# Other instruction durations in the scheduler of a two-layer hybrid trunk

## The chip, the cores and the metric

The kernel runs on one core of a Trainium2 chip. The metric is the device time of one execution in microseconds (us). The engines are TensorE (PE in the profile, its weight loads PEld), VectorE (DVE), ScalarE (ACT), GpSimd (POOL) and SyncE (SP), which issues all loads and stores.

## The reference

Two decoder layers over 512 tokens of 1024 features, all in float32. `rms_norm`, `rope`, `indexer`, `attention` and `mlstm` stand here for the reference's functions:

```
for i in range(2):
    xn = rms_norm(h, g_mix)
    c_q, k, v, k_idx, w_idx, mq, mk, mv, mo, mi, mf = split(xn @ w_in)
    c_q = rms_norm(c_q, g_cq)
    q, q_idx = rope(rms_norm(c_q @ w_q_up, g_qn)), rope(c_q @ w_iq_up)   # 8 heads of 64 each
    k, k_idx = rope(rms_norm(k, g_kn)), rope(rms_norm(k_idx, g_ik))
    score = sum over 8 heads of w_idx * relu(q_idx . k_idx), causal       # indexer
    sel   = the 128 best keys of each query by score
    att   = softmax(q . k over sel / 8) @ v                               # 8 heads, 2 kv heads
    hm    = sigmoid(mo) * rms_norm(mlstm(silu(conv(mq)), silu(conv(mk)), mv, mi, mf), g_mh)
    h = h + concat(att, hm) @ w_out
    h = h + relu(rms_norm(h, g_mlp) @ w_ff1) ** 2 @ w_ff2
    h = h + sigmoid(rms_norm(h, g_ple) @ w_ple_gate + b) * (p[i] @ w_ple)
return h
```

## The kernel before

The residual stream `h` stays on chip, feature-major, in eight tiles of 128 features by 512 tokens. Each float32 operand of a large product is split into a leading part (`hi`, made by ScalarE) and a remainder (`lo`, by VectorE, or for some weights by GpSimd if that is idle), both in float32r, and a product runs as three passes: hi x hi, hi x lo, lo x hi. Products of attention values, of the mLSTM and of sums of squares run in plain float32, which the trace shows as two matmul records each.

A weight tile is 128 x 1024. It is loaded by SyncE into `raw` (3 places), split into `hi` and `lo` (4 places each), and used for 24 products of 512 columns. In the trace, `lo<-raw,hi` is the remainder of a weight, `ps_proj` and `ps_up` are accumulators of projections, `ps_tr` of transposes and small sums, `ps_sc` of scores, `ps_po` of attention values, `ps_pn` of mLSTM values.

A layer's first part, `mix`, makes the compressed queries, then keys and gates, then the index queries and queries (`up`, 42 products of 512 columns a layer), whose norms (`headnorm`, lines 656 to 674) end with a gain that GpSimd multiplies in (`s<-s,const`, 128 x 512), followed by rope on VectorE and by `stack`, which splits them (`s_sp`) and has TensorE transpose them. From the index scores VectorE picks the 128 best keys in 16 rounds of MAX8 and MATCH_REPLACE8 for each of three query blocks. The mLSTM's values and output gates (label `values`, 192 products in one fixed order) and its queries and keys (label `conv`, eight blocks of 24 products) need none of that; they are what TensorE can do meanwhile. Then come attention, mLSTM, the output product in two halves, the MLP with 1536 products and the gated input.

No order is written out by hand. Class `Plan` records all instructions with their dependencies. `schedule` (lines 239 to 361) then simulates the five engines: whenever an engine is idle it takes, of the instructions that are ready and whose results have a place, the one with the highest rank. A rank is the longest chain of durations (`cost`, lines 199 to 227) and hops between engines (`lag`) behind the instruction, plus a fixed number of microseconds for its part of the work (`URGENT`); an earlier stage always goes first. An instruction that is offered to two engines goes to the one that is idle. The order in which this simulation issues the instructions is the program: each engine's queue executes in that order, and an instruction that is not ready holds up all behind it. So `cost` makes no instruction faster or slower; it moves instructions against one another.

The lines of `cost` for TensorE, where n is the number of columns and `single` means float32r:

```
if method == "transpose":
    return 56.0 if single else 109.0
return max(107.0, n / 2.4 + 3) if single else max(214.0, n / 0.6 + 3)
```

Of the kernel before, what the change touches and what calls it, by code (L numbers as in the profile page):

```python
"""Two layers of a hybrid trunk: top-k sparse attention next to mLSTM heads, squared-relu MLP, gated per-layer input.

The residual stream stays in SBUF, feature-major, for the whole program; every weight is read once.
A float32 product runs as three float32r passes: each operand is split exactly into a leading part of
12 significant bits and a remainder, and only the product of the two remainders (below float32's last bit)
is left to rounding.
"""
# [17 lines left out]
S = 512  # L25
# [10 lines left out]
# 500000 ** (-2 i / 16) in float32  # L36
INV_FREQ = (1.0, 0.1939227432012558, 0.03760603070259094, 0.007292664609849453, 0.0014142135623842478,
            0.00027424818836152554, 5.3182957344688475e-05, 1.0313385246263351e-05)
# columns of the feature-major constants
C_MIX, C_MLP, C_PLE, C_BPLE, C_CQ, C_CB, C_CW, C_MH, NCF = 0, 8, 16, 24, 32, 34, 42, 74, 78  # L40
# columns of the token-major constants
T_K, T_Q, T_I, T_F, NCT = 0, 192, 256, 260, 264
# tiles of the weight stream of one layer
W_CQ, W_UP, W_QK, W_V, W_O, W_OUT, W_FF1, W_FF2, W_PLE, W_GATE, NW = 0, 2, 4, 12, 16, 20, 28, 60, 92, 94, 102

# places of a room that must stay free behind an instruction that takes one
MARGIN = {"s": 5, "pw": 10, "out0": 0, "out1": 0, "mlstm": 8, "conv": 3}
# the first loads, in us of urgency from one to the next; the weights of the compressed queries come behind AHEAD of them
STEP, AHEAD = 5, 8
# how much more urgent a part of the work is than the length of the chain behind it says, in us  # L50
# [5 lines left out]
class View:  # L56
    """A part of a buffer, recorded: the steps that lead to it, and the elements it covers."""
# [25 lines left out]
    def split(self, inner):  # L83
        """[p, (a b)] -> [p, a, b] with b = inner."""
        return self._with(("rearrange", "p (a b) -> p a b", inner), self.index.reshape(-1, inner))

    def flat(self):
        """[p, a, b] -> [p, (a b)]."""
        return self._with(("rearrange", "p a b -> p (a b)", None), self.index.reshape(-1))
# [37 lines left out]
class Plan:  # L127
    """Records the program's instructions, chooses the order in which the engines issue them, and issues them.

    The order is that of a list scheduler: an idle engine takes, of the instructions whose operands are there and  # L130
    whose results have a place, the one with the longest chain of work behind it."""
# [16 lines left out]
    def add(self, forms):  # L148
        """forms: the instruction, possibly for several engines: (engine, method, args, kwargs)."""
# [48 lines left out]
    @staticmethod  # L198
    def cost(form):
        engine, method, args, kw = form  # L200
        out = kw["out"] if "out" in kw else args[0]
        views = [v for v in list(args) + list(kw.values()) if isinstance(v, View)]
        if engine == "sync":
            v = out if isinstance(out, View) else views[0]
            return 60.0 + v.index.size * v.shape[0] * 4 / 357.0
        n = max(v.index.size for v in views if v is not kw.get("accum_out"))
        columns = [v for v in views if v.index.size == 1 and n > 1]
        inputs = [v for v in views if v is not out and v.index.size > 1]
        bank = any(v.buf.room == "ps" for v in views)
        if engine == "tensor":  # L210
            single = (args[1] if len(args) > 1 else kw["lhsT"]).buf.dtype == F32R
            n = out.index.size
            if method == "transpose":
                return 56.0 if single else 109.0
            return max(107.0, n / 2.4 + 3) if single else max(214.0, n / 0.6 + 3)
        if engine == "scalar":
            return (51 if bank else 93) + n * 0.834 + 93 * len([v for v in columns if v is not out]) \
                + (0 if "accum_out" in kw and kw["accum_out"] is not None else 0)
        if engine == "gpsimd":
            return 100 + n * {"tensor_tensor": 2.25, "memset": 0.5, "affine_select": 1.0}.get(method, 1.4)  # L220
        if method == "reciprocal":
            return 69 + 6.25 * n
        if method == "tensor_tensor_scan":
            return 69 + 2.08 * n
        if method in ("tensor_copy", "tensor_scalar") and not bank and "accum_out" not in kw:
            return 69 + n * 0.52 + (61 if columns else 0)
        return 69 + n * 1.042 + (61 if columns and method == "scalar_tensor_tensor" else 0)

    @staticmethod
    def lag(a, b):  # L230
        """From the end of an instruction of engine a to the start of one of engine b that needs it."""
        if a == b:
            return {"vector": 110.0, "scalar": 60.0, "gpsimd": 100.0}.get(a, 0.0)
        if b == "sync":
            return 1220.0
        if a == "sync":
            return 900.0
        return 320.0 if b == "tensor" else 200.0 if a == "tensor" else 150.0
# [127 lines left out]
    def issue(self, nc, tc, pools):  # L366
        """pools: per room the Tile pool; a room without a number of places gives each buffer its own."""
# [25 lines left out]
class Trunk:  # L393
# [19 lines left out]
    def setup(self):  # L413
# [9 lines left out]
        # triu[s, t] = 1 where s <= t  # L423
# [3 lines left out]
        # cmask[q, s] = 0 where s <= q, else -1e30  # L427
# [4 lines left out]
        # negsel[r, h, :] = -1 where r == h  # L432
# [24 lines left out]
    def rope_tables(self):  # L457
        """cc = (cos, cos), sn = (-sin, sin) of position * inv_freq, token-major [128, 4, 16]."""
# [53 lines left out]
    def weight(self, ap, cols=1024, pool=False):  # L512
        """Loads a weight tile and splits it; returns (hi, lo)."""
# [16 lines left out]
    def rsqrt(self, v, shape):  # L530
        """v ** -0.5 of a tiny positive tile, to float32 accuracy."""
# [15 lines left out]
    def prep(self, l, gcol):  # L547
        """Splits h * gain per feature block and gathers the tokens' sums of squares."""
# [22 lines left out]
    def token_r(self, acc, dim):  # L571
        """acc [128 features, S] of squares -> [128 tokens, NTB] rsqrt(mean + eps)."""
# [14 lines left out]
    def wide_r(self, acc, dim):  # L587
        """acc [128 features, S] of squares -> rsqrt(mean + eps) of every token, on every partition, [128, S]."""
# [16 lines left out]
    def spread(self, r):  # L605
        """[128 tokens, NTB] -> the same value on every partition, [128, S]."""
# [18 lines left out]
    def mm3(self, out, w, x, first, last):  # L625
        """out += w^T x, w and x given as (hi, lo)."""
        nc = self.nc
        head = nc.tensor.matmul(out, w[0], x[0], start=first, stop=False)
        nc.tensor.matmul(out, w[0], x[1], start=False, stop=False)
        return head, nc.tensor.matmul(out, w[1], x[0], start=False, stop=last)  # L630

    def token_step(self, o, w, cols, x, k, per, tb, first, last):
        """o [128 tokens of block tb, cols] += x_k^T w_k; a tile w holds `per` k-blocks."""
# [7 lines left out]
    def rope(self, x, heads, blocks=range(NTB)):  # L641
        """In place on the first 16 dims of x: per token block [128, heads, 64]."""
# [13 lines left out]
    def headnorm(self, x, heads, gain, per_head):  # L656
        """x: per token block [128, heads, 64] (in place): rms norm of each head, times gain."""
# [18 lines left out]
    def stack(self, y, tb, outs):  # L676
        """y [128 tokens of block tb, 8 heads, 64] -> outs[head][:, block]: the leading parts of the 64 dims on
        partitions 0..63, the remainders on 64..127."""
# [18 lines left out]
    def doubled(self, x, heads):  # L697
        """x: per token block [128, heads, 64] -> per head (hi, lo) tiles [128, S], the 64 dims twice on the
        partitions."""
# [17 lines left out]
    def blocks(self, ws, xs, t=slice(0, S)):  # L717
        """Blocks of 128 output features side by side; the last feature block of x comes last."""
# [7 lines left out]
    def mix(self, l):  # L726
# [6 lines left out]
        # compressed queries  # L733
# [33 lines left out]
        # keys, values, indexer key and weights, gates  # L767
# [19 lines left out]
        # index queries and queries  # L787
# [52 lines left out]
        # gates of the mLSTM, token-major [128, NTB, 4]  # L840
# [22 lines left out]
        # log1p(z) = 2 y (1 + lp)  # L863
# [4 lines left out]
        # before[tb] = sum of the blocks ahead of tb  # L868
# [26 lines left out]
        # values and output gates of the mLSTM, token-major  # L895
# [21 lines left out]
        # mLSTM queries and keys: convolution over tokens, silu (times two)  # L917
# [18 lines left out]
        # attention  # L936
# [113 lines left out]
    def out_half(self, l, half, cat):  # L1050
        """Adds a half of the output product (0: mLSTM, 1: attention) to the residual stream."""
# [12 lines left out]
    def inputs(self, l, i, raws):  # L1064
        """Half of the product of the per-layer input, for the end of the layer; fills gaps of the tensor engine."""
# [69 lines left out]
    def ple(self, l):  # L1135
# [7 lines left out]
        for n0, cnt in ((0, 2), (2, 1), (3, 1), (4, 1), (5, 1), (6, 1), (7, 1)):  # L1143
            ws = [self.wtile(l, W_GATE + n0 + j) for j in range(cnt)]
            # the very last block in two halves of the tokens: less is left to do behind its last product
# [51 lines left out]
def col_blocks(w):  # L1197
    """[l, K, N] -> [l, N/128, 128, K]: per block of 128 columns, the rows of each 128-row block side by side."""
# [4 lines left out]
def row_pairs(w):  # L1203
    """[l, K, N] -> [l, K/256, 128, 2 N]: two 128-row blocks side by side."""
# [4 lines left out]
def out_pairs(w):  # L1209
    """[l, 512, 1024] -> [l, 4, 128, 1024]: two blocks of 128 columns side by side, each with its 128-row blocks."""  # L1210
    return col_blocks(w).reshape(L, 4, 2, 128, 512).transpose(0, 1, 3, 2, 4).reshape(L, 4, 128, 1024)


def columns(v):
    """[l, N] -> [l, 128, N/128]."""
# [42 lines left out]
```

## Time and profile before

| | |
|---|---|
| Time, median of 3 runs | 1372.2 us (1370.88 to 1372.2) |
| Span of the profiled execution, from its first to its last instruction | 1370.7 us, 1.5 us less than the median |
| TensorE busy | 1333.6 us, 97% |
| VectorE, ScalarE, GpSimd busy | 887.2, 554.8, 188.1 us |
| Loaded and stored | 116.40 MB, mean 85 GB/s |
| Chain that ended last | TensorE 88%, VectorE 8%, ScalarE 2% |

All instructions carry line 381, where `issue` calls them, so they are told apart by their tiles. Busy time of TensorE is modelled with overlapping ends: one 512-column product is shown as some 390 ns long, while the next starts 231 ns after it. Starts are therefore the better measure of its pace. The two layers have the same plan, and what stands at 72 us in layer 0 stands at 748 us in layer 1.

### The profile page before, as it was taken

To read this page: it belongs to the slowest core of one execution; us is meant where nothing else is said; L and a number is where in the kernel's file an instruction comes from. 1 tells how busy PE (TensorE), PEld (TensorE's weight loads), DVE (VectorE), ACT (ScalarE), POOL (GpSimd) and SP (SyncE) were. 2 spreads that over 40 slices of the span, in tenths; PEclk is the share of its full clock that TensorE was granted. 3 is DMA by queue.
4 is the path that set the end of the run, shared out by engine and by line. 5 is a ranking of instruction groups with operands and counts; after the bars stand their busy time and mean duration, and the time that the engine had idled before them with its cause. 6 is when DMAs were issued, how large, how long until landed. Compare 5 with 4: busy or idle time off the path is not lost.

```text
span 1370.7 us, 17012 instructions
## 1 busy us (share of the span) xinstructions
PE 1333.6 (97%) x6336; PEld 1096.2 (80%) x6336; DVE 887.2 (65%) x1791; ACT 554.8 (40%) x1106; POOL 188.1 (14%) x151
## 2 busy tenths in 40 slices
PE   7979999999999999999998899999999999999998
PEld 6767889888888888888896778988888888888887
DVE  7989998575354453554859999966743534535454
ACT  4765486332122221234546644844222212222441
POOL 4244200120000000012104341003100000000210
PEclk9989999999999999999999899999999999999999
DMA  5212211333333233333231123103223233323321
GB/s 189 70 55 78 92 32 32 93 92 92 96 95 101 93 92 92 93 100 96 80 90 50 66 83 93 32 21 102 93 93 93 93 97 99 97 93 92 95 83 69
DMA packets 34355, 116.40 MB, mean 85 GB/s; under 512 B 4192, under 2 KB 4704, under 8 KB 34272
## 3 DMA queue, kind: packets, MB, share of 16 engines
q1 hardware_dynamic: 34272, 115.32, 27.4%
q8 instruction: 49, 0.80, 0.2%
q14 instruction: 34, 0.28, 0.1%
HBM read 113.21 MB, written 2.10 MB: 84 GB/s over the span
## 4 chain that ended last, share of the span: by engine, by line
PE 88%; DVE 8%; ACT 2%; issue 1%; DMA 1%; POOL 0%; SPq 0%; ACTq 0%; DVEq 0%; POOLq 0%
PE ps_proj L381 78%; PE ps_sc L381 3%; PE ps_tr L381 3%; DVE s L381 3%; PE ps_po L381 2%; PE ps_pn L381 1%; ACT s L381 1%; DVE s_w L381 1%; DVE wide L381 1%; DVE s_sp L381 1%; DVE m L381 1%; DVE tiny L381 1%; DVE lo L381 0%; POOL s L381 0%; DMA raw<-wa 0%
## 5 line engine op out<-in xcount | busy, mean ns | idle before, releaser
L381 PE MATMUL ps_proj<-s,hi 128*128 128x512 f32 x2960 | 920.1, 393 | 0.4 <-ACT hi L381 0.4
L381 PEld LDWEIGHTS ps_proj<-s,hi 128*128 128x128 f32 x2960 | 554.3, 188 | 127.0 <-issue 1.8
L381 PE MATMUL ps_proj<-s,lo 128*128 128x512 f32 (+1 forms) x1480 | 576.9, 393 | 0.3 <-DVE lo L381 0.3
L381 ACT ACTIVATE hi<-raw 128x1024 fp32r<-128x1024 f32 (+1 forms) x212 | 222.4, 1052 | 646.2 <-PE ps_proj L381 317.3
L381 PEld LDWEIGHTS ps_proj<-s,lo 128*128 128x128 f32 x1480 | 278.2, 188 | 64.1 <-DVE lo L381 0.7
L381 DVE TENSOR_TENSOR lo<-raw,hi 128x1024 fp32r<-128x1024 f32 (+1 forms) x181 | 223.2, 1234 | 33.9 <-ACT hi L381 30.9
L381 DVE TENSOR_TENSOR const<-const,ps_proj 128x512 f32<-128x512 f32 x96 | 66.0, 688 | 224.3 <-PE ps_proj L381 224.3
L381 POOL TENSOR_TENSOR lo<-raw,hi 128x1024 fp32r<-128x1024 f32 x31 | 75.6, 2442 | 531.9 <-ACT hi L381 525.0
L381 DVE SCALAR_TENSOR_TENSOR s_v<-ps_proj,s 128x512 f32<-128x512 f32 x64 | 43.9, 691 | 138.3 <-PE ps_proj L381 138.3
L381 POOL TENSOR_TENSOR s<-s,s 128x512 f32<-128x512 f32 x42 | 68.3, 1626 | 411.5 <-ACT s L381 297.0
L381 PE MATMUL ps_proj<-hi,s 128*128 128x512 f32 (+1 forms) x384 | 112.4, 381 | 7.2 <-ACT hi L381 7.2
L381 PE MATMUL ps_sc<-s,s 128*128 128x384 f32 (+3 forms) x288 | 85.4, 382 | 0.0
L381 PEld LDWEIGHTS ps_proj<-hi,s 128*128 128x128 f32 x384 | 69.3, 194 | 16.3 <-ACT hi L381 7.2
L381 PE MATMUL ps_proj<-lo,s 128*128 128x512 f32 (+1 forms) x192 | 66.5, 385 | 1.9 <-DVE lo L381 1.9
L381 PEld LDWEIGHTS ps_sc<-s,s 128*128 128x128 f32 x288 | 52.5, 195 | 9.4 <-issue 3.1
L381 ACT ACTIVATE s<-ps_tr 128x128 fp32r<-128x128 f32 (+2 forms) x170 | 38.9, 307 | 34.4 <-PE ps_tr L381 34.1
L381 DVE MATCH_REPLACE8 s<-m,s 128x384 f32<-128x384 f32 (+2 forms) x96 | 51.2, 537 | 0.0
L381 DVE TENSOR_TENSOR s<-s_vv,s 128x512 fp32r<-128x512 f32 x64 | 49.2, 773 | 0.2
L381 PE MATMUL ps_po<-at,s_et 128*128 128x64 f32 x320 | 48.9, 254 | 0.0
L381 DVE MAX8 m<-s 128x8 f32<-128x384 f32 (+2 forms) x96 | 48.8, 542 | 0.0
L381 PEld LDWEIGHTS ps_po<-at,s_et 128*128 128x128 f32 x320 | 47.8, 191 | 1.1
L381 DVE SCALAR_TENSOR_TENSOR s<-const,const,s 128x512 fp32r<-128x512 f32 x48 | 39.8, 833 | 11.5 <-ACT s L381 11.4
(133 smaller groups left out, 1105.0 us busy)
## 6 DMA issues: line engine op xcount, KB each, us to landing
raw<-ws SPq DMA_DIRECT2D x204, 512.0 KB, 3.5
raw<-wa SPq DMA_DIRECT2D x8, 336.0 KB, 3.4
const<-xt SPq DMA_DIRECT2D x8, 256.0 KB, 4.7
out<-const SPq DMA_DIRECT2D x7, 256.0 KB, 2.0
s<-pt SPq DMA_DIRECT2D x4, 256.0 KB, 4.1
const<-ct SPq DMA_DIRECT2D x2, 132.0 KB, 4.2
out<-const SPq DMA_DIRECT2D x2, 128.0 KB, 1.7
const<-cf SPq DMA_DIRECT2D x2, 39.0 KB, 2.7
```

Source lines behind the costliest of these rows:

```text
L381: ins = getattr(getattr(nc, e), method)(*[value(x) for x in args], **{k: value(x) for k, x in kw.items()}).ins
```

## The change

Six numbers in `cost` are changed. Nothing else that acts is: comments and docstrings have become blank lines, so line numbers stay.

```
         if engine == "tensor":
             ...
             if method == "transpose":
-                return 56.0 if single else 109.0
-            return max(107.0, n / 2.4 + 3) if single else max(214.0, n / 0.6 + 3)
+                return 60.0 if single else 109.0
+            return max(111.0, n * 0.4375 + 7) if single else max(172.0, n * 1.66 + 11)
         ...
         if engine == "gpsimd":
-            return 100 + n * {"tensor_tensor": 2.25, "memset": 0.5, "affine_select": 1.0}.get(method, 1.4)
+            return 100 + n * {"tensor_tensor": 2.4, "memset": 0.8, "affine_select": 1.0}.get(method, 1.4)
```

## Rows read from the trace of the kernel before

**Rows 1.** The page: busy time, share of the span and instructions of each engine.

```profile
span 1370.7 us, 17012 instructions
PE 1333.6 (97%) x6336; PEld 1096.2 (80%) x6336; DVE 887.2 (65%) x1791; ACT 554.8 (40%) x1106; POOL 188.1 (14%) x151
```

**Rows 2.** Busy time by stage: stretch, length, engines' busy us, clock, DMA share, GB/s.

```profile
0.00:20.00 20.00, 10.96 (x55) 10.01 (x56) 15.58 (x14) 15.18 (x24) 14.82 (x24) 1.00 0.66 209
20.00:40.00 20.00, 19.28 (x94) 16.35 (x93) 14.02 (x66) 6.04 (x9) 0.00 (x0) 0.91 0.41 123
...
73.00:80.00 7.00, 0.00 (x0) 0.00 (x0) 7.00 (x4) 0.00 (x0) 5.68 (x3) 0.71 0.30 81
80.00:130.00 50.00, 47.18 (x222) 37.58 (x222) 47.09 (x122) 30.69 (x86) 18.34 (x13) 0.94 0.24 73
130.00:165.00 35.00, 35.00 (x155) 27.82 (x156) 33.09 (x84) 17.20 (x28) 13.59 (x11) 1.00 0.29 91
165.00:235.00 70.00, 70.00 (x506) 63.01 (x505) 65.79 (x224) 51.98 (x167) 3.39 (x8) 1.00 0.11 31
235.00:675.00 440.00, 440.00 (x1902) 356.46 (x1901) 231.22 (x280) 133.18 (x168) 34.22 (x21) 1.00 0.31 93
...
911.00:1366.00 455.00, 454.69 (x1994) 370.56 (x1992) 234.69 (x288) 130.18 (x164) 30.59 (x18) 1.00 0.29 91
1366.00:1371.00 5.00, 0.00 (x0) 0.00 (x0) 1.00 (x3) 0.51 (x1) 0.00 (x0) 0.85 0.09 31
```

**Rows 3.** The chain that ended last, in order of time: start us, us, what.

```profile
221.24 2.23 PE ps_pn L381 x20
...
284.21 361.49 PE ps_proj L381 x1560
```

**Rows 4.** TensorE in order of time, around its long wait in either layer.

```profile
72.55 0.40 PE L381 MATMUL ps_proj<-lo,s 128*128 128x512 f32 x1
80.14 0.62 PE L381 MATMUL ps_tr<-const,s_sp 128*128 128x128 f32 x3 [7.19 <-DVE s L381]
...
755.57 0.62 PE L381 MATMUL ps_tr<-const,s_sp 128*128 128x128 f32 x3 [7.22 <-DVE s L381]
```

**Rows 5.** VectorE in order of time, layer 0.

```profile
64.03 2.29 DVE L381 TENSOR_TENSOR wide<-wide,wide 128x32 f32<-128x32 f32 x1
66.36 0.19 DVE L381 SCALAR_TENSOR_TENSOR wide<-wide,wide 128x32 f32<-128x32 f32 x1
...
71.60 1.30 DVE L381 TENSOR_TENSOR s_w<-s,const 128x64 f32<-128x64 f32 x1 [1.17 <-POOL s L381]
...
74.11 2.35 DVE L381 TENSOR_TENSOR s_w<-s,const 128x64 f32<-128x64 f32 x1
```

**Rows 6.** GpSimd in order of time, layer 0.

```profile
63.85 2.42 POOL L381 TENSOR_TENSOR lo<-raw,hi 128x1024 fp32r<-128x1024 f32 x1 [10.35 <-ACT hi L381]
68.88 5.16 POOL L381 TENSOR_TENSOR s<-s,const 128x512 f32<-128x512 f32 x3 [2.60 <-DVE tiny L381]
73.99 4.69 POOL L381 TENSOR_TENSOR lo<-raw,hi 128x1024 fp32r<-128x1024 f32 x2
```

**Rows 7.** TensorE by stage, layer 0: products into ps_proj alone, then ps_up alone.

```profile
40.00:73.00 33.00, 17.36 (x66) 1.00 0.24 75
80.00:130.00 50.00, 37.12 (x138) 0.94 0.24 73
...
40.00:73.00 33.00, 9.95 (x42) 1.00 0.24 75
```

**Rows 8.** TensorE's short waits, 80 to 130 and 756 to 806 us: total, times, longest.

```profile
PE ps_tr L381 <- DVE s_sp L381: 2.7, 3, 1.3
...
PE ps_tr L381 <- DVE s_sp L381: 2.6, 3, 1.3
```

**Rows 9.** GpSimd's groups from 60 to 130 us: busy us, mean ns | idle before.

```profile
L381 POOL TENSOR_TENSOR lo<-raw,hi 128x1024 fp32r<-128x1024 f32 x9 | 21.8, 2431 | 38.1 <-ACT hi L381 34.6 <-issue 3.4
L381 POOL TENSOR_TENSOR s<-s,const 128x512 f32<-128x512 f32 x4 | 6.5, 1637 | 3.2 <-DVE tiny L381 2.6 <-DVE s L381 0.6
```

## The prediction

> **What bounds the kernel now.** I read the totals of the page first, then the busy time by stage, then the chain of waits, then the three engines around the one place where TensorE stands. The totals show TensorE busy for 97% of the span [rows 1]. The stages show where the other 3% lie [rows 2]: TensorE is full from 130 to 716 us and again from 806 to 1366 us, and is short only in the first 40 us, at 40 to 130 us (layer 0, indexer) and at 716 to 806 us (the same in layer 1). In a full stretch the order of the instructions can't matter: 1560 products of 512 columns take 361.49 us, 231.7 ns each, whatever lies between them [rows 3]. So the change is worth what it does in the two indexer stretches, and there VectorE is full: 7.00 of 7 us while TensorE does nothing, 47.09 of the 50 after it.
>
> At 72.9 us TensorE's queue reaches transposes whose operands VectorE has not made, and waits 7.19 us; 675 us later it waits 7.22 us in the same place [rows 4]. The work behind them in the queue can't pass. VectorE is late because of GpSimd: a 128x32 TENSOR_TENSOR takes 2.29 us where its neighbour of that size takes 0.19 us, and small ones after it take 1.30 and 2.35 us [rows 5]. Each of the long ones lies over a GpSimd TENSOR_TENSOR: three gains of the queries for 5.16 us from 68.88, and two remainders of weights for 4.69 us behind them [rows 6]. The scheduler's table has no such stretching: 69 + 32 x 1.042 is 102 ns for that 2.29 us instruction. So the plan believes VectorE faster than it is.
>
> The Trainium skill (SBUF — State Buffer, section "SBUF: two separate sides") says that VectorE instructions with two SBUF inputs and GpSimd ones lock each other out for a whole instruction. The 2.29 us agree. By that rule the block's 9.85 us (5.16 + 4.69) are lost to such VectorE instructions wherever it stands, so a split block only spreads the wait and the sum stays at the +3.0 us below; by the rows alone, where two blocked instructions take 1.3 us only, a split could give up to the 7.2 us of the wait back. The chance of that case is set from the rows.
>
> **The change part by part.** No instruction is added or removed, so its direct cost is zero; everything is in the order, on all five queues. SyncE's loads only follow the plan, and DMA has room (a share of at most 0.41 after the first 20 us [rows 2]).
>
> *TensorE, 512-column float32r products: 216.3 to 231 ns.* The new figure is what the trace has (231.7 ns), the old one 15 ns short. The cover it gave: the scheduler hands TensorE a fill product whenever nothing more urgent is ready, and an instruction that needs VectorE enters the queue when the plan thinks VectorE done. With products too short by 6%, the plan put 6% more of them ahead of every such instruction, and on the chip that excess absorbed part of VectorE's unplanned delay. With the true figure fewer stand ahead, while VectorE's delay, which the table still doesn't know, stays. So TensorE arrives at the blocked transposes earlier and waits longer, and the displaced products come later. How much: from 40 to 73 us the trace has 66 products into ps_proj and 42 into ps_up, and 138 into ps_proj from 80 to 130 [rows 7]. At 14.7 ns each (231 - 216.3; a few have 336 columns and move by 11) that is 1.6 us before the long wait and 2.0 us between the short waits behind it, 3.6 us in layer 0 at most. Layer 1 runs the same plan, so the upper end is 7.2 us for both. Lower end nothing: the short waits after the stall, 2.7 and 2.6 us [rows 8], and those before it could swallow the displaced products. Below nothing this term by itself can't go, since it only takes fill away. I take the middle, 3.6 us, as the long waits, three quarters of the waiting, can't be refilled behind the blocked head and the short ones partly can.
>
> *GpSimd: 2.25 to 2.4 ns an element.* 512 columns go from 1252 to 1329 ns, 1024 from 2404 to 2558; the trace has 1637 for the gains and 2431 for the remainders between 60 and 130 us [rows 9]. The plan now sees what waits for GpSimd later: 0.08 us for each of 4 gains, 0.15 for each of 9 remainders, 1.7 us a layer if all were in one chain. This works against the first term (the dependents move back in the queues), but few lie in one chain with TensorE's waits. Bounds -1.7 to 0 us a layer; I take -0.3, or -0.6 in all, by the three gains that run before the long wait (0.23 us).
>
> *TensorE, float32.* Products of 64 columns or fewer go from 214 to 172 ns, 128-column ones from 216 to 223.5, 129 from 218 to 225 (trace: 20 records, two a product, in 2.23 us, 223 ns [rows 3]). These run where TensorE is full, 165 to 235 us [rows 2], so no wait moves directly; cost zero. What could go wrong there: VectorE is also nearly full (65.79 of 70 us), and attention put later could leave TensorE without work before the output product. Bounds 0 to +3 us a layer, by the size of the short waits; I take 0.
>
> *Urgencies.* The scheduler orders by the longest chain behind an instruction. The chain of mLSTM values has 192 products a layer, so its head gains 192 x 14.7 = 2.8 us; the queries lose up to 80 x 42 = 3.4 us from the chain of attention products and regain 0.6 us from the scores. So weights for the fill products move up by some 3 to 6 us against the queries, which can change which of a remainder and a gain GpSimd runs first. This is the part I can't follow to the end: it can merge or split the block of five GpSimd instructions. From the row, the most at stake in a layer is the long wait, 7.2 us, plus what the halved clock after it costs: the granted clock averages 0.94 over the 50 us from 80 [rows 2], which is 6 us at 1.2 GHz and so 3 us of work. Bounds -10 to +7 us a layer; I take 0, since the block is made of the same instructions released in the same chain.
>
> *Start and end.* The first 40 us lose 9 and 0.7 us to loads and first splits [rows 2], and the last 5 us have no product left; order changes little there: bounds -1 to +1 us, taken as 0.
>
> Sum: 3.6 - 0.6 = +3.0 us on the profiled span of 1370.7 us. The median of the runs shown is 1372.2, 1.5 us above the span; I carry that along: 1370.7 + 1.5 + 3.0 = 1375.2, rounded to 1375.
>
> **The rivals.** A difference below 0.2% (2.7 us) can't be told from no change here.
>
> First rival, nothing measurable: the waits are set by VectorE and GpSimd, whose order in the stretch stays, and the displaced products fall into the short waits. For it: the two layers repeat the wait to 0.03 us [rows 4], so it is made by the dependency chain. Against it: VectorE works at its limit for 100 us, so a displaced product has no idle time guaranteed. 1370 to 1375; centre 1372.
>
> Second rival, faster: the changed urgencies let a weight's remainder run before the gains, or spread the gains, so that the block of five GpSimd instructions breaks, VectorE's instructions slip through and the long wait halves in both layers: -7.2 us, 1365. It decides from the point where one GpSimd remainder moves out of the ten microseconds after 68.88 us; if the wait goes entirely and the clock stays up, 2 x 10 = 20 us, 1352. For it: the values move up by as much as the queries go down. Against it: the remainders wait for ScalarE's leading parts (38.1 us of GpSimd's idle time [rows 9]), so urgency alone doesn't bring them earlier.
>
> Third rival, clearly slower: the block grows by another remainder (2.4 us a layer) and attention finishes late, 3 us a layer: 2 x 5.4 = 11 on top of the 3, 1386. For it: VectorE is full up to 235 us. Against it: TensorE shows no wait there now.
>
> **How the numbers follow.** Forecast, slower by 0.2 to 0.7%: 0.36, with 1375. Nothing measurable: 0.27. Faster: 0.29, most of it from 1362 to 1369. Clearly slower: 0.08. So faster 0.29, same 0.27, slower 0.44. The range of 8 in 10 runs from 1362 (leaving out a tenth, where the long waits vanish) to 1385 (leaving out the upper part of the third rival); the forecast's own range is 1375 to 1382.
>
> **What would show it.** Right: both long waits of TensorE for VectorE are still there, near 8 us each, at the same kind of transposes, fewer products into ps_proj stand before them, GpSimd runs gains and remainders back to back, and full stretches keep 231 to 232 ns a product. The first term is wrong if the long waits get shorter while the GpSimd block is unchanged; the rival of the urgencies is right if the block is split and the clock no longer falls behind it. The whole is wrong if a wait appears where TensorE is full now, at 130 to 716 or 806 to 1366 us, or if the start moves by more than a microsecond.

## The result and the profile after

The changed kernel takes 1417.76 us (1417.67 to 1420.34, 4 runs) against 1372.2 us: the ratio is 1.0337, 95% interval 1.0322 to 1.0351. That is 45.6 us slower, where 3 us slower and a range up to 1385 us were forecast.

First the totals of the page, as in [rows 1]:

```profile
span 1416.0 us, 17028 instructions
PE 1354.8 (96%) x6336; PEld 1103.7 (78%) x6336; DVE 911.1 (64%) x1807; ACT 551.7 (39%) x1096; POOL 185.1 (13%) x145
```

TensorE's idle time has grown from 37.1 to 61.2 us. The other 21 us stand as busy time of the same 6336 products; part of it is time at the halved clock, for which an estimate stands below. Next the busy time by stage, columns as in [rows 2]; the indexer stretch is one window here:

```profile
20.00:40.00 20.00, 16.27 (x85) 13.96 (x86) 13.99 (x67) 6.16 (x9) 0.00 (x0) 1.00 0.34 110
40.00:130.00 90.00, 77.63 (x385) 61.39 (x383) 86.49 (x238) 54.10 (x161) 34.90 (x19) 0.96 0.22 68
130.00:165.00 35.00, 35.00 (x147) 26.55 (x146) 35.00 (x88) 16.35 (x28) 15.31 (x14) 1.00 0.28 91
165.00:190.00 25.00, 20.74 (x102) 15.16 (x100) 24.87 (x52) 13.53 (x29) 1.08 (x2) 1.00 0.24 67
190.00:240.00 50.00, 48.35 (x350) 44.41 (x350) 40.63 (x147) 33.90 (x113) 1.47 (x5) 0.93 0.07 21
240.00:262.00 22.00, 17.82 (x96) 14.17 (x96) 11.46 (x40) 7.81 (x25) 0.13 (x1) 0.84 0.00 1
```

Four of these windows of the kernel before, the first one the indexer stretch again (20 to 40 and 130 to 165 us stand in [rows 2]):

```profile
40.00:130.00 90.00, 78.28 (x386) 62.52 (x385) 85.12 (x245) 57.15 (x165) 35.60 (x24) 0.94 0.24 75
165.00:190.00 25.00, 25.00 (x147) 21.10 (x146) 24.93 (x82) 18.01 (x56) 2.08 (x4) 1.00 0.14 43
190.00:240.00 50.00, 50.00 (x385) 45.97 (x385) 43.72 (x149) 35.57 (x115) 1.31 (x4) 1.00 0.08 22
240.00:262.00 22.00, 22.00 (x97) 17.85 (x96) 11.00 (x13) 5.21 (x7) 0.00 (x0) 1.00 0.32 97
```

The reader is to see that the indexer stretch, on which the prediction was built, has hardly more idle time (12.4 us against 11.7), and that the loss stands behind it, at 165 to 262 us, where TensorE was full before and is now idle 10.1 us. The 3.0 us more of idle time from 20 to 40 us make nothing late: the last product of the keys, with which that part ends, starts at 42.2 us before and 42.7 after. Layer 1 has the same picture 700 us later.

Matching each product of the two traces by its place in the program gives the sizes in layer 0. The last product of the mLSTM values starts at 131.1 us before and 134.2 after (+3.1). The last attention product starts at 231.6 and 242.2, so 7.5 us more were lost on the way. The first MLP product starts at 277.9 and 300.1, so another 11.6 us were lost. In layer 1 `mix` takes 263.7 us before and 287.0 after: +23.3, beside +22.2. Outside `mix` nothing has changed: the long stretch of products keeps its pace of [rows 3], 231.5 ns each, in the chain that ended last:

```profile
306.18 361.59 PE ps_proj L381 x1562
```

What TensorE waits for in the new places is in the view of its waits from 165 to 262 us (total, times, longest); before, this view has no line:

```profile
PE ps_sc L381 <- DVE s L381: 2.7, 1, 2.7
PE ps_tr L381 <- DVE s_hn L381: 2.5, 1, 2.5
PE ps_sc L381 <- DVE s_d L381: 2.4, 3, 1.0
```

The cause is fill that is left over: work that TensorE could do while it waits, done too late to serve for that. Products into ps_proj in two stretches of layer 0, before and then after; up to 230 us these are the conv blocks:

```profile
165.00:190.00 25.00, 14.09 (x56) 1.00 0.14 43
190.00:230.00 40.00, 0.00 (x0) 1.00 0.10 28
```

```profile
165.00:190.00 25.00, 12.35 (x44) 1.00 0.24 67
190.00:230.00 40.00, 9.64 (x24) 0.91 0.04 12
```

Before, all conv blocks are done at 188 us, when attention gets going. After, the last block of 24 products is still to do at 190 us and, ranked below attention, is scattered between its products until 221.6 us. The fourth mLSTM head needs that block. Its products into ps_pn move from 221 to 243 us, behind the last attention product, and its norm, which before lay under attention, now has only the first products of the output half beside it.

This order is made by the plan and not first on the chip. In TensorE's queue 35 of layer 0's 240 attention instructions stand ahead of the last conv product before, 130 in the changed kernel. `schedule` itself, run on the old table, never leaves TensorE idle in layer 0's `mix` and starts the last conv product at 152 us of its own clock. Run on the new one, it starts that product at 185 us and leaves TensorE idle for 5.3 us between the last values product and the last attention product and for 5.9 us behind it, 11.2 us in all. The simulation knows nothing of VectorE's stretched instructions [rows 5], so idle time of this size needs none of them.

TensorE in order of time around that norm:

```profile
250.03 0.40 PE L381 MATMUL ps_proj<-s,lo 128*128 128x512 f32 x1
252.96 1.16 PE L381 MATMUL ps_tr<-const,s_hn 128*128 128x128 f32 x4 [2.53 <-DVE s_hn L381]
254.90 1.58 PE L381 MATMUL ps_proj<-s,hi 128*128 128x512 f32 x2 [0.78 <-ACT s L381]
...
259.26 1.05 PE L381 MATMUL ps_proj<-s,hi 128*128 128x512 f32 x2
...
260.51 0.63 PE L381 MATMUL ps_proj<-s,hi 128*128 128x512 f32 x2
```

The gaps are small, but after them the granted clock falls to the 1.2 GHz level (0.84 as a mean of the 22 us): a pair of products takes 1.05 us there, and 0.63 us once the clock is back at 260.5 us. By the clocks of the table above, 0.93 over 50 us and 0.84 over 22 us, the halved clock takes up to 7.0 us a layer from 190 to 262 us, an estimate; with the 10.1 us of idle time that is most of the 19.1 us lost behind the values.

### The profile page after: what moved, and what is told of

It is laid out like the page before. It is cut to its first block, busy times and chain, and to the rows that moved or that the text cites. A ratio compares the mean times of both kernels' runs of the same rounds, so it can differ in the third digit from the quotient of the medians.

```text
span 1416.0 us, 17028 instructions
## 1 busy us (share of the span) xinstructions
PE 1354.8 (96%) x6336; PEld 1103.7 (78%) x6336; DVE 911.1 (64%) x1807; ACT 551.7 (39%) x1096; POOL 185.1 (13%) x145
## 4 chain that ended last, share of the span: by engine, by line
PE 78%; DVE 17%; issue 2%; ACT 2%; DMA 1%; POOL 0%; SPq 0%; DVEq 0%; ACTq 0%; POOLq 0%
PE ps_proj L381 69%; DVE s L381 8%; DVE m L381 3%; PE ps_sc L381 3%; PE ps_tr L381 2%; PE ps_po L381 2%; DVE s_sp L381 2%; PE ps_pn L381 1%; DVE tiny L381 1%; DVE wide L381 1%; DVE lo L381 1%; ACT hi L381 0%; DVE s_d L381 0%; ACT s L381 0%; DVE s_t L381 0%
## 5 line engine op out<-in xcount | busy, mean ns | idle before, releaser
L381 PEld LDWEIGHTS ps_proj<-s,hi 128*128 128x128 f32 x2960 | 555.9, 189 | 131.1 <-ACT s L381 3.0
L381 DVE TENSOR_TENSOR lo<-raw,hi 128x1024 fp32r<-128x1024 f32 (+1 forms) x185 | 227.1, 1229 | 33.1 <-ACT hi L381 30.1
L381 PE MATMUL ps_proj<-hi,s 128*128 128x512 f32 (+1 forms) x384 | 115.3, 385 | 7.3 <-ACT hi L381 7.3
L381 PE MATMUL ps_sc<-s,s 128*128 128x384 f32 (+3 forms) x288 | 88.9, 398 | 14.2 <-DVE s L381 5.4
L381 POOL TENSOR_TENSOR lo<-raw,hi 128x1024 fp32r<-128x1024 f32 x27 | 67.6, 2503 | 106.5 <-ACT hi L381 98.2
L381 ACT ACTIVATE s<-ps_tr 128x128 fp32r<-128x128 f32 (+2 forms) x170 | 39.1, 310 | 37.1 <-PE ps_tr L381 37.1
L381 PEld LDWEIGHTS ps_po<-at,s_et 128*128 128x128 f32 x320 | 50.7, 203 | 2.6
L381 DVE MAX8 m<-s 128x8 f32<-128x512 f32 (+2 forms) x96 | 48.8, 543 | 0.0
L381 ACT ACTIVATE s<-const,const 128x512 fp32r<-128x512 f32 x48 | 34.2, 714 | 29.7 <-DVE const L381 27.8
```

The lines of the kernel that those rows point to most:

```text
L381: ins = getattr(getattr(nc, e), method)(*[value(x) for x in args], **{k: value(x) for k, x in kw.items()}).ins
```

## The experiments

The table's values are used twice: for the ranks (the chain behind an instruction) and for the simulated clock (when an engine is free again). The first two runs take these apart. Both give `cost` a second argument:

```
 c = min(self.cost(f, RANK) for f in op.forms)      # e1: new table, e2: old
 op.end = now + self.cost(op.form, CLOCK)           # e1: old table, e2: new
```

> The new durations are used for the ranks alone (the chains of work behind an instruction), the old ones for the simulated clock. Theory A, pace: the harm comes from the simulated clock, which lets TensorE do fewer fill products (values, conv) before attention is ready; then attention, which ranks higher, pushes the last conv blocks and the last mLSTM heads behind it. By A this kernel is near the kernel before: 1366 to 1382 us, the last products of the fourth mLSTM head (ps_pn) before the last of attention (ps_po). Theory B, urgency: the changed chain lengths alone reorder conv, mLSTM and attention; by B this kernel is near the changed one, 1405 to 1425 us.

Measured: 1378.03 us, ratio 1.0041 (1.0028 to 1.0055).

> The mirror: old durations for the ranks, new ones for the simulated clock. Theory A, pace: near the changed kernel, 1400 to 1430 us, with the last ps_pn behind the last ps_po and a stretch of halved clock at the end of mix in both layers. Theory B, urgency: near the kernel before, 1366 to 1382 us.

Measured: 1435.43 us, ratio 1.0459 (1.044 to 1.0478), above the 1430 expected; the last ps_pn of layer 0 starts at 259.7, behind the last ps_po at 255.1, but in layer 1 it doesn't (962.9 against 965.6). So the simulated clock makes the loss, and the new ranks take some 18 of its 63 us back. Urgency falls as the main cause; alone it costs about 6 us.

The third run gives conv and mLSTM their place back by hand, the fourth is its control on the old table:

```
-          "attention": -20, "mlstm": 20, "out0": -115, "out1": -145}
+          "attention": -30, "mlstm": 20, "out0": -115, "out1": -145}
```

> The changed kernel with one number more: attention's urgency is -30 instead of -20 us, so conv and mLSTM go ahead of attention again. If the loss lies where the traces put it (per layer 3 us by the end of the values, 7.5 us from there to the last attention product, 11.5 us from there to the end of the output product), this gives the last two back in both layers, 2 x 19 = 38 us: 1380 us, 1372 to 1388. If instead VectorE's stretching in the indexer stretch is the loss, attention's urgency does little: 1405 to 1420.

Measured: 1403.74 us, ratio 1.0224 (1.0209 to 1.0239): 14 us back, not 38, a miss. By the matched products the last term is gone in both layers: from the last attention product to the first MLP product it is 46.4 us, as before (46.3), where the changed kernel has 57.9. The middle term stays (in layer 0, 109.0 us from the last values product to the last attention product, before 100.5, changed 108.0), and the first grows to 6.4 us. The stretch 165 to 190 us shows why: TensorE still waits while VectorE is full, now without a pause:

```profile
165.00:190.00 25.00, 22.26 (x104) 17.33 (x103) 25.00 (x41) 12.24 (x22) 4.29 (x5) 1.00 0.19 51
```

So the end of `mix` is a matter of who goes last and can be mended by an urgency; this one did not mend the middle.

> Control: the kernel before with attention's urgency at -30. There conv ends before attention anyway, so by theory A little changes: 1366 to 1380 us. If -30 by itself is worth tens of microseconds (1345 or less), the third run says nothing about where the changed table loses.

Measured: 1375.22 us, ratio 1.002 (1.0011 to 1.0029). The urgency by itself is worth nothing on the old table, so the 14 us belong to the changed one.

Next, one line of the table at a time:

> Only the line for float32r products is new (231 instead of 216.3 ns for 512 columns), the rest of the table is old. Theory A, pace: TensorE's simulated pace against the other engines is what counts, so this alone brings most of the loss: 1400 to 1440 us, with the conv blocks ending after attention has begun. Theory C, any disturbance: every order but the one that the constants were picked for loses tens of microseconds, whichever number is changed; then it lies by chance between 1380 and 1430 and the next three runs of this set lie there too.

Measured: 1432.88 us, ratio 1.0435 (1.0415 to 1.0456).

> Only the line for float32 products is new (172 instead of 214 ns for 64 columns and fewer). Theory A: attention values become cheaper in the simulation, which makes TensorE's simulated pace a little faster over a part of mix, so little is lost: 1370 to 1390 us. Theory C: 1380 to 1430 us.

Measured: 1379.87 us, ratio 1.0069 (1.0048 to 1.009). The float32r line alone brings more than the whole change; the others together soften it. The float32 line by itself costs 8 us where the prediction had zero. The GpSimd line and the transposes were not run alone. Theory C, that any other order loses tens of microseconds, doesn't hold: this run and the two further ones of its set, below, lose 8, 0 and 2 us with orders that differ from the one before.

The next one keeps the float32r line new and makes the other engines in the simulation slower by the same factor:

```
 def cost(form):
+    c = Plan.cost0(form)
+    return c if form[0] == "tensor" else c * 1.068
 ...
-    op.rank += 1000.0 * (URGENT...)
+    op.rank += 1068.0 * (URGENT...)
```

and likewise `lag`, `HOP` and the constants of the clock model. TensorE's transposes and float32 products keep their old durations.

> The new line for float32r products, and every other duration of the simulation but TensorE's (VectorE, ScalarE, GpSimd, SyncE, the hops, the urgencies) raised by the same 6.8%. TensorE's pace against the others is then that of the kernel before, while the durations are no truer or less true. Theory A: the loss goes: 1366 to 1382 us. Theory C, or a theory by which the longer TensorE durations harm as such: 1390 or more.

Measured: 1371.42 us, ratio 1.0 (0.9991 to 1.001). The loss is gone. The number 231 does no harm by itself; 231 beside old durations and old urgencies does. Which of these it clashes with, this run can't tell, as all were scaled at once.

Is the loss graded? Two sizes between 216.3 and 231 ns, `n / 512 * 222` and `n / 512 * 225`:

> A float32r product of 512 columns at 222 ns, 39% of the way from 216.3 to 231. If the loss grows with the number of fill products displaced, as the prediction had it, it is 39% of what e5_f32r_only loses, about 15 to 25 us: 1387 to 1397. If there is a point from which conv no longer ends before attention takes over, and 222 lies before it, nearly nothing of the loss shows: 1370 to 1383.

Measured: 1374.11 us, ratio 1.0018 (1.0009 to 1.0027).

> A float32r product of 512 columns at 225 ns, 3 ns above the 222 that lost 2 us and 6 below the 231 that lost 61. If there is a point from which the last conv blocks fall behind attention, this order has passed it (its last conv product comes after the second query block of attention values, as in the changed kernel): 1395 to 1435 us. If the loss is graded between 222 and 231, a third of 59 us: 1390 to 1398. If the point lies higher: 1372 to 1380.

Measured: 1405.96 us, ratio 1.0252 (1.0239 to 1.0266). Between 222 and 225 ns the time rises by 32 us, more than half of the 61 us that 231 ns costs (e5). Products into ps_proj from 190 to 230 us, at 222 and at 225:

```profile
190.00:230.00 40.00, 0.00 (x0) 1.00 0.09 28
```

```profile
190.00:230.00 40.00, 9.36 (x24) 1.00 0.08 24
```

Between them the left-over conv block appears, all 24 products of it. In the other kernels the same count is 0 in the kernel before, e1, e4 and e8 (1371 to 1378 us), 13 in e6 (1380), 15 in e3 (1404), 24 in the changed kernel, 22 in e2 (1435) and 29 in e5 (1433): a sign of the loss, though not its size. The idle time that `schedule` itself leaves TensorE in `mix` orders them much alike, but for e3: in both layers together at most 6.7 us in the kernel before, e1, e4, e8 and e9, 7.5 in e3, 7.9 in e6, 13.7 in e13, 22.6 in the changed kernel, 30.4 in e5 and 34.9 in e2.

Last, the other side of the balance. The gains of `headnorm` go to VectorE, on the changed table:

```
-            nc.gpsimd.tensor_tensor(x[tb], x[tb], g, op=ALU.mult)
+            nc.vector.tensor_tensor(x[tb], x[tb], g, op=ALU.mult)
```

> The changed kernel with the gains of headnorm multiplied by VectorE instead of GpSimd (16 instructions in all, 8 of 512 columns for the queries and 8 of 192 for the keys; VectorE gets some 0.6 us of work for each of the 8). Those gains are what held VectorE up in the trace of before. If VectorE's unplanned delay is the other half of the mechanism (TensorE waits because the plan takes VectorE for faster than it is), then with part of that delay gone the true TensorE durations do much less harm: 1375 to 1400 us. If TensorE's pace alone decides, it stays at 1410 to 1425.

Measured: 1374.47 us, ratio 1.0016 (1.0007 to 1.0026), just below the 1375 to 1400 expected. One line gives 43 of the 45.6 us back with the true TensorE durations in place. In the changed kernel the four gains and the next remainder hold GpSimd for 13.8 us on end (in order of time, to be read with [rows 6]):

```profile
73.92 11.01 POOL L381 TENSOR_TENSOR s<-s,const 128x512 f32<-128x512 f32 x4 [1.08 <-DVE s L381]
84.89 2.85 POOL L381 TENSOR_TENSOR lo<-raw,hi 128x1024 fp32r<-128x1024 f32 x1
```

and VectorE's instructions beside them are stretched as in [rows 5]. One over that remainder, and its like behind it:

```profile
85.40 2.76 DVE L381 SCALAR_TENSOR_TENSOR s<-s_idx,wide,s 128x384 f32<-128x384 f32 x1
...
89.48 0.61 DVE L381 SCALAR_TENSOR_TENSOR s<-s_idx,wide,s 128x384 f32<-128x384 f32 x1
```

With the edit that block is gone, as is the left-over block (no product into ps_proj from 190 to 230 us). But the edit also puts this work on VectorE in the simulation, so the plan sees VectorE later and the order moves: `schedule` starts the last conv product of layer 0 at 160 us instead of 185 and leaves TensorE idle for 3.1 us instead of 11.2. So the changed plan by itself takes the left-over block away; whether less exclusion on the chip adds to the gain, this run can't tell.

Two candidates with the same edit on the old table:

> A candidate to beat both: the kernel before with the gains on VectorE, the float32r transpose at 60 ns and the gates' urgency at 55 instead of 75. The long wait of 7.2 us in either layer should shrink, VectorE has 4 x 0.6 us more a layer: 1364 to 1370 us; 1372 if the wait only moves.

Measured: 1371.67 us, ratio 1.0004 (0.9995 to 1.0013), no gain.

> Another candidate: the kernel before with the gains on VectorE and the urgency of the values at 25 instead of 30. Same expectation: 1364 to 1370 us; 1372 if the wait only moves.

Measured: 1369.81 us, ratio 0.9985 (0.9976 to 0.9994): the only version whose interval lies ahead of the kernel before, by 2.6 us, less than 0.2%. TensorE's waits on VectorE, two of 7.2 us before, are now two of 4.5 (total, times, longest):

```profile
PE ps_tr L381 <- DVE s L381: 9.0, 2, 4.5
```

## Why the prediction was wrong

**The place.** That "the change is worth what it does in the two indexer stretches", since "in a full stretch the order of the instructions can't matter", is the step that failed. A stretch is full as long as there is fill for it, and the order decides when the fill is used up. From 130 to 235 us [rows 2] TensorE was full because conv lasted to 188 us, just until attention could take over. Float32 work in that stretch was priced at "cost zero", bounds 0 to +3 us a layer; the stretch and the output product behind it cost 19 us a layer, 10.1 us of it in waits where TensorE had none. The prediction named the sign: wrong as a whole if a wait appears between 130 and 716 us. The clue stood in the same rows: VectorE at 65.79 of 70 us, so nothing but the order of the fill kept TensorE from waiting for it.

**The size.** "At 14.7 ns each" priced a displaced product by its own duration and bounded the first term by 7.2 us for both layers. Up to the end of the values the size came near: 3.1 us in layer 0, 4.8 in layer 1, where 1.8 was taken and 3.6 the upper end. That is luck in part, as the way was another. Fewer products into ps_proj were to stand before the long wait; there are more, 74 by 73 us against 66 in [rows 7], since the first values product starts at 42.9 us instead of 50.6:

```profile
40.00:73.00 33.00, 19.37 (x74) 1.00 0.28 88
```

Behind the values the loss isn't a sum over products: e9 and e13 show a step of 32 us for 3 ns. Once attention is ready before the last conv block, its rank pushes the block back by 34 us, and mLSTM's chain with it.

**The mechanism.** Too short a TensorE duration was to serve as cover for VectorE's unplanned delay, which the true figure would uncover on the chip. The runs show another way to the loss: e1 and e2 put it on the simulated clock, e8 on the ratio of TensorE to the rest of the simulation, and `schedule` has the left-over block and 11.2 us of idle TensorE with no unplanned delay at all. That GpSimd holds VectorE up is in the rows of the two engines; whether this delay has a part in the 45.6 us stays open. In e10 the plan moved along with it, and with the gains off GpSimd on the old table (e11, e12) no more than 2.6 us were gained. For a part speaks e3, which loses 31 us where its plan has 7.5 us of idle TensorE, and waits while VectorE is full.

**The long waits.** They were to stay "near 8 us each". They are gone, and shorter waits of about the same sum stand in their place: TensorE is idle 12.4 us from 40 to 130 us, 11.7 before. Its two longest groups of waits there now (total, times, longest):

```profile
PE ps_tr L381 <- DVE s_sp L381: 5.5, 4, 2.0
PE ps_tr L381 <- DVE s L381: 1.7, 1, 1.7
```

So the long wait, taken for the heart of the matter, could go without the time going with it. The second rival had expected 1352 to 1365 us from just that.

**GpSimd and the urgencies.** The urgencies, taken as 0 with bounds -10 to +7 us a layer, cost 5.6 us in both layers together (e1). The GpSimd line, -0.6 us in the sum, was not run alone. The third rival, 1386 us by a grown GpSimd block and a late attention, came nearest: attention ends 11 us later, where it had 3, and the block lasts 13.8 us instead of 9.8, though by a fourth gain in place of a remainder. It lacked the largest part, the 11.6 us behind the last attention product.

## What to carry to other kernels

In a planner, what counts is the ratio of the engines' durations, and of the urgencies set beside them, not the truth of one of them: one truer number can make the plan worse. So change them together, or scale the rest as in e8. Before a run, ask the planner itself where the engine that bounds the kernel is idle in its new plan: here it showed 11 us a layer in place of none, in the second half of `mix`, while the prediction looked only at the waits of the old trace. Where two engines are both full, look at what fill is left when the next urgent work becomes ready, and at what would then end last; that margin can have a step in it, and a linear estimate doesn't reach across. A run with a third of the change and one with two thirds shows such a step.

## What was not expected of the hardware

The exclusion between GpSimd and VectorE works both ways, and who is in possession can keep the other out for several instructions. In the changed kernel GpSimd's third gain takes 5.33 us and its fourth 1.29 us, GpSimd first and then VectorE in order of time:

```profile
78.34 5.33 POOL L381 TENSOR_TENSOR s<-s,const 128x512 f32<-128x512 f32 x1
83.64 1.29 POOL L381 TENSOR_TENSOR s<-s,const 128x512 f32<-128x512 f32 x1
```

```profile
79.25 0.67 DVE L381 TENSOR_TENSOR s<-s,wide 128x512 f32<-128x512 f32 x1
79.85 0.73 DVE L381 SCALAR_TENSOR_TENSOR s<-s_idx,wide,s 128x512 f32<-128x512 f32 x1
80.51 0.41 DVE L381 TENSOR_TENSOR s_sp<-s,s_sp 128x256 fp32r<-128x256 f32 x1
80.85 0.73 DVE L381 SCALAR_TENSOR_TENSOR s<-s_idx,wide,s 128x512 f32<-128x512 f32 x1
...
82.18 0.34 DVE L381 TENSOR_TENSOR s_w<-s,const 128x64 f32<-128x64 f32 x2
```

Here VectorE runs one instruction behind the other until 82.5 us, and the gain, four times as long as its neighbour, ends 1.2 us after that; in [rows 5] it was VectorE that stood. The Trainium skill (SBUF — State Buffer, "SBUF: two separate sides") says that of the two, whichever starts first holds the shared ports for its whole instruction and the other blocks. The trace agrees in both directions; that a run of short instructions keeps the other engine out longer than any one of them lasts is what I had not expected.
